# Two-layer hybrid diffusion block: modulation sums tied to the product's pace, rotary tables moved into the FFN, branch A's keys and queries first

## The chip, the cores and the metric

The kernel runs on one core of a Trainium2 chip. The metric is device time in microseconds (us), lower is better. Five engines work side by side, each in its own order: TensorE (PE in the profile) multiplies, VectorE (DVE) and ScalarE (ACT) do elementwise work, GpSimd (POOL) does small elementwise work and copies, SyncE (SP) issues the DMAs.

## The reference, cut to what matters

Two layers over 256 latent and 256 context tokens of width 1024. Each layer is an FFN half step, three token mixers, and a second FFN half step; every norm is modulated by sums over the conditioning vector.

```python
for l in range(DEPTH):                       # 2
    mx = split(silu(c) @ ada_w[l] + ada_b[l], 9)       # modulation of the latents, mz alike of the context
    x = x + 0.5 * mx[2] * swiglu(adaln(x, ffn1_norm, mx[0], mx[1]), ffn1_w_in, ffn1_w_out)   # z alike
    u = adaln(x, mix_norm, mx[3], mx[4])               # A: windowed GQA, B: global GQA, C: latent attention
    ya, yb, yc = A(u), B(u), C(u)                      # queries and keys: rms norm per head, gains, rotary
    m = sigmoid(ga) * (ya @ w_a) + sigmoid(gb) * (yb @ w_b) + sigmoid(gc) * (yc @ w_c)
    x = x + mx[5] * (m @ w_out)
    x = x + 0.5 * mx[8] * swiglu(adaln(x, ffn2_norm, mx[6], mx[7]), ffn2_w_in, ffn2_w_out)
return x                                     # the last layer's second half does the latents only
```

## The kernel before

All 512 tokens are the columns of every product (256 in the last layer's second part). An fp32 product is three passes on TensorE (`mm3`, L101 to L103): each operand is split into a high part (ACT, L108) and a low part (DVE, L109). Weights come as chunks of 512 KB, two chunks ahead; every second one goes into a `q4` buffer, whose load waits for a one-element copy on GpSimd (L154).

TensorE's order is written by hand in the code's order of products; the order of the other engines comes from the framework's scheduler, and each engine runs its instructions strictly in that order.

An FFN half step (`ffn`, `residual`) makes the 22 row blocks of the hidden layer in three splits (7, 7, 8). A row block is a gate and an up product, 24 TensorE products of 512 columns each. `evac` then takes them out: silu on ACT, L495 on DVE (h = silu x up), the high half on ACT (L108, `m<-w`), the low half on DVE (L109, `m<-w,m`). After each split, `residual` multiplies its row blocks by the output weights and adds into x (L427); after the last split it also sums squares for the next norm (ACT L355, DVE L356), whose sum over channels is TensorE's L372.

The modulation of later stages is made under three of the FFNs (`ada`): a step loads 128 rows of `ada_w` (L249, 512 KB, tiles `pth` and `ptl`) and sums them against the conditioning with one DVE instruction per stream (L266, 128x1024, two per step, 224 in all; the FFN of layer 0 does 48 steps). A step comes after every 29 or 44 TensorE products (`PACE`). The load is issued three steps ahead of its use (`ADA_LOOK`) and waits for a copy on GpSimd (L248) of `self.pace`, an element of the newest low half of the hidden layer or of x. The sums themselves carry no such tie: the scheduler decides where they stand on DVE.

The mixer starts with `rope_tables` (loads of the gains, L580 and L584; DVE L585 to L599; GpSimd L594 and L606). Then come the keys and values of A and B (`prep_kv`: split of V, preparation of A's keys, of B's keys), then A's queries. `k_heads` (L666 on TensorE, L671 and L673 to split) turns keys, `q_heads` (L683) queries; scores are L706, the probabilities are turned by L750. A filler (gates and other branches' products) is handed out in estimated us by the table `FILLS` between these steps: `keys` before A's keys are turned, `start` before attention, `a` and `b` between scores.

Of the kernel before, what the change touches and what calls it, by code (L numbers as in the profile page):

```python
# [9 lines left out]
ALU = mybir.AluOpType  # L10
# [16 lines left out]


FILLS = (
    dict(a=2.0, b=1.7, keys=0.0, start=8.0, latent=2.0, ups=5.0, c0=9.0, c=2.5),  # L30
    dict(a=2.0, b=1.8, keys=7.5, start=8.0, latent=0.0, ups=2.0, c0=0.0, c=1.3),
)
ADA_LOOK = 3
DEPTH_AB, DEPTH_C = 3, (2, 3)
# [24 lines left out]
class Kernel:  # L59
# [171 lines left out]
    def ada(self, mods):  # L231


        nc = self.nc
        cb = self.T("m5", [128, 2, D])
        for i in range(2):
            nc.gpsimd.tensor_copy(out=cb[:, i, 0:1], in_=self.pace)
        nc.sync.dma_start(out=cb, in_=self.t["condb"])
        nc.scalar.activation(out=cb, in_=cb, func=AF.Silu)
        junk = self.T("m6", [128, 2, D])  # L240
        todo = [(l, m, j) for l, m in mods for j in range(KD)]
        raws = []

        def load():
            n = len(raws)
            if n < len(todo):
                raw = self.T(("pth", "ptl")[n % 2], [128, D], bufs=2)
                nc.gpsimd.tensor_copy(out=raw[:, 0:1], in_=self.pace)  # L248
                nc.sync.dma_start(out=raw, in_=self.t["ada_t"][todo[n]])  # L249
                raws.append(raw)  # L250


        for _ in range(ADA_LOOK):
            load()
        yield
        n = 0
        for l, m in mods:

            streams = 1 if l == DEPTH - 1 and m > 4 else 2
            o = self.mods[l][:, m]  # L260
            for j in range(KD):
                load()
                raw = raws[n]
                n += 1
                for i in range(streams):
                    nc.vector.scalar_tensor_tensor(  # L266
                        out=junk[:, i], in0=raw, scalar=1.0, in1=cb[:, i], op0=ALU.mult, op1=ALU.mult,
                        accum_out=o[:, j, i:i + 1])
                if j < KD - 1:
                    yield  # L270
            b = self.adab[:, l, m].unsqueeze(2).to_broadcast([128, KD, streams])
            nc.vector.tensor_tensor(out=o[:, :, :streams], in0=o[:, :, :streams], in1=b, op=ALU.add)
            self.set_gains(l, m, slice(0, KD), streams)
            yield
# [204 lines left out]
    def ffn(self, l, f, halves, fill, after):  # L479
# [18 lines left out]
        for si, (t0, nt) in enumerate(SPLITS):  # L498
            hid = [[self.T(f"m{i}", [128, 4, NT], F32R) for i in ii] for ii in ((0, 1), (3, 4))]
            i0 = 0  # L500
            if si == 0:
                held = []
                i0 = len(halves)
                for i in range(i0):
                    tag = self.turn()
                    held.append([(self.P(tag), self.chunk("ffn_in", (f, l, t0 + i, gu), 1024)) for gu in range(2)])
                if self.first:
                    self.first(sum(held, []), rhs)
                    self.first = None
                    for i in range(i0):  # L510
                        evac(i, hid, held[i][0][0], held[i][1][0], whole)
                else:
                    for half in halves:

                        for k in range(KD):
                            for acc, wt in sum(held, []):
                                self.col_product(wt, KD, rhs, acc, HALF[half], (k, k + 1))
                            if k % 2:
                                self.tick()
                        for i in range(i0):  # L520
                            evac(i, hid, held[i][0][0], held[i][1][0], HALF[half])
                        self.finish()
            for i in range(i0, nt):
                accs = []
                tag = self.turn()
                for gu in range(2):
                    acc = self.P(tag)
                    self.col_product(self.chunk("ffn_in", (f, l, t0 + i, gu), 1024), KD, rhs, acc, whole)
                    accs.append(acc)
                    if gu == 0:  # L530
                        fill(24)
                evac(i, hid, accs[0], accs[1], whole)
                self.pace = hid[1][i // 4][:, i % 4, 0:1].bitcast(F32)
                fill(24)
            hrhs = [[hid[s][k // 4][:, k % 4] for k in range(nt)] for s in range(2)]

            def weights(d, t0=t0, nt=nt):
                return self.chunk("ffn_out", (f, l, d, slice(None), slice(t0, t0 + nt)), nt * 128)

            final = si == len(SPLITS) - 1  # L540
            self.residual(l, n, weights, nt, hrhs, halves, final, fill, after if final else None)
# [104 lines left out]
        elif rq is None:  # L646
            self.gain_heads(t, c0, nh, 64)

    def prep_kv(self, raw):
        V = self.V = self.T("m6", [128, 4, 4, 128], F32R)  # L650
        for tt in range(4):
            v = raw[tt][:, 256:512].rearrange("p (h d) -> p h d", h=4)
            self.split(V[:, tt, :, 0:64], V[:, tt, :, 64:128], v)
        for b, c0 in enumerate((G_AK, G_BK)):
            if b:
                self.rope_tables64((c0,))
            for tt in range(4):
                self.prep_heads(raw[tt][:, b * 128:(b + 1) * 128].rearrange("p (h d) -> p h d", h=2), c0, tt, 2)

    def k_heads(self, raw, b):  # L660

# [126 lines left out]
                    lambda g=g, i=i: [v[g * 64:g * 64 + 64, i, HALF[half]] for v in y],  # L788
                )

    def attention(self, steps, preps, fill, depth):


        n = len(steps)
# [2 lines left out]
        for k in early:  # L797
            for f in preps[k]:
                f()
        for i in range(min(depth, n)):  # L800
            fill()
            steps[i][0]()
# [203 lines left out]
    def mixer(self, l, last, after):  # L1006
# [11 lines left out]
                self.tick()  # L1018
            self.finish()

        self.rope_tables(l)

        nc.scalar.activation(out=self.small("go", 1), in_=self.hh[:, KD - 1, 0:1].bitcast(F32), func=AF.Exp, scale=0.0)
        self.rq = [self.T(f"rq{b}", [128, 4, 8]) for b in range(3)]
# [7 lines left out]
        for k in range(KD):  # L1032
            s = self.dram.tile([128, NT], F32, name=f"xd{l}_{k}")
            nc.sync.dma_start(out=s[:, :nh], in_=self.x[k][:, whole])
            xd.append(s)
        self.prep_kv(g3)
        aq = self.T("m3", [128, 4, 512])
        aq = [aq[:, tt] for tt in range(4)]
        drain(self.tok_product(l, "w_aq", 512, 2, aq, qtts))
        for tt in qtts:  # L1040
            self.prep_heads(aq[tt].rearrange("p (h d) -> p h d", h=8), G_AQ, tt, 8, self.rq[0][:, tt])
        self.share = 3
        depth = DEPTH_AB
        y = [[self.T(f"m{i}", [128, 4, NT], F32R) for i in (0, 1)], []]
# [16 lines left out]
        def fill():  # L1061
            def gates(ds):
                for d in ds:
                    m.append(self.T(f"x{d}", [128, NT]))
                    yield from self.gate_tanh(l, 0, d, whole, m[d][:, whole])

            yield from gates(range(2))
            self.K[1] = self.k_heads(g3, 1)
            self.rope_tables64((G_BQ,))
            yield from gates(range(2, 4))  # L1070
            bq.extend(self.raw4(512))
            yield from self.tok_product(l, "w_bq", 512, 2, bq, qtts, "d")
            left = list(qtts)
# [32 lines left out]
        fill(us["keys"])  # L1106
        self.K[0] = self.k_heads(g3, 0)
        fill(us["start"] - us["keys"])
        self.attention(steps, preps, lambda: fill(us["a"] if self.at < na else us["b"]), depth)
        t3 = [self.T("q4", [128, 2, NT], F32R, bufs=Q4) for _ in range(3)]  # L1110
        qT = [[t3[s][:, 0], t3[s][:, 1], t3[2][:, s]] for s in range(2)]
        while not have:
# [265 lines left out]
```

## Time and profile before

| | before |
|---|---|
| median of 3 runs | 2191.96 us (2191.35 to 2192.39) |
| profiled execution, its own time | 2207.8 us |
| its span | 2206.0 us |
| TensorE busy | 2118.2 us (96%) |
| VectorE busy | 1490.1 us (68%) |
| ScalarE busy | 991.6 us (45%) |
| GpSimd busy | 523.0 us (24%) |
| mean granted TensorE clock | 0.985 |

The span is the time from the first to the last instruction. By the first instruction of each stage the FFN of layer 0 runs from about 29 to 416 us, its mixer to 928, its second FFN to 1300, the first FFN of layer 1 to 1663, its mixer to about 2006, and the last FFN to the end.

### The profile page before, as it was taken

Reading aid. Unit: us, or ns where it says so; the run is one execution under the profiler, and the core shown is the slowest. Engines: PE = TensorE matmul, PEld = TensorE weight load, DVE = VectorE, ACT = ScalarE, POOL = GpSimd, SP = SyncE. Lnnn points to the kernel's source line nnn. Section 1 sums busy time; section 2 is a strip of 40 time slices with the busy share of each in tenths; the row PEclk is TensorE's granted clock in tenths of the full one; section 3 lists DMA queues with packets and bytes.
Section 4 is the critical chain, followed back from the end, with each engine's and each line's share of the span. In section 5 each row is a group of like instructions: output and inputs, shape, how many; then the busy total and the mean of one; then the engine's idle time right before and its main releaser. Section 6 shows DMA issues by size and latency. Waiting matters only on the chain. (4 is left out here: it accounts for less than half of the span.)

```text
span 2206.0 us, 33338 instructions
## 1 busy us (share of the span) xinstructions
PE 2118.2 (96%) x11832; PEld 1840.0 (83%) x11832; DVE 1490.1 (68%) x3041; ACT 991.6 (45%) x2026; POOL 523.0 (24%) x806
## 2 busy tenths in 40 slices
PE   6999998999999999999999999999999799899999
PEld 3878787878898888988878898787887799799999
DVE  5676666678888665657665466755557978887665
ACT  4322222456775664432223343222235676675554
POOL 3100010365335431201000021010115633721000
PEclk9999999999999999999999999999999899999999
DMA  8554454331112213345544325455552332335554
GB/s 288 181 178 162 164 180 140 115 96 49 51 50 86 85 58 125 106 139 177 166 148 154 113 77 185 168 168 167 173 169 95 121 99 83 102 125 188 185 184 124
DMA packets 95526, 299.16 MB, mean 136 GB/s; under 512 B 10880, under 2 KB 15616, under 8 KB 94976
## 3 DMA queue, kind: packets, MB, share of 16 engines
q1 hardware_dynamic: 95360, 297.04, 41.4%
q8 instruction: 93, 1.52, 0.3%
q14 instruction: 73, 0.60, 0.1%
HBM read 292.80 MB, written 4.19 MB: 135 GB/s over the span
## 5 line engine op out<-in xcount | busy, mean ns | idle before, releaser
L108 ACT ACTIVATE whi<-raw 128x512 fp32r<-128x512 f32 (+2 forms) x521 | 310.0, 609 | 340.9 <-PE pd L102 96.5
L109 DVE TENSOR_TENSOR wlo<-raw,whi 128x512 fp32r<-128x512 f32 (+2 forms) x441 | 304.8, 695 | 87.5 <-ACT whi L108 85.7
L101 PE MATMUL pd<-hh,whi 128*128 128x512 f32 (+1 forms) x864 | 306.4, 355 | 3.3 <-ACT hh L408 1.9
L102 PE MATMUL pd<-hl,whi 128*128 128x512 f32 (+1 forms) x864 | 303.7, 352 | 0.9 <-DVE hl L409 0.9
L103 PE MATMUL pd<-hh,wlo 128*128 128x512 f32 (+1 forms) x864 | 302.8, 350 | 0.0
L108 ACT ACTIVATE whi<-q 128x512 fp32r<-128x512 f32 (+1 forms) x299 | 179.3, 615 | 230.2 <-PE pd L102 67.3
L154 POOL COPY q<-start 1x1 f32<-1x1 f32 x151 | 63.1, 418 | 818.8 <-DVE wlo L109 623.5
L109 DVE TENSOR_TENSOR wlo<-q,whi 128x512 fp32r<-128x512 f32 (+1 forms) x299 | 200.1, 673 | 79.4 <-ACT whi L108 78.2
L266 DVE SCALAR_TENSOR_TENSOR m<-ptl,m 128x1024 f32<-128x1024 f32 x112 | 134.5, 1222 | 165.2 <-DMA ptl<-ada_t 165.1
L266 DVE SCALAR_TENSOR_TENSOR m<-pth,m 128x1024 f32<-128x1024 f32 x112 | 134.6, 1222 | 159.4 <-DMA pth<-ada_t 144.7
L108 ACT ACTIVATE m<-w 128x512 fp32r<-128x512 f32 (+1 forms) x92 | 51.5, 560 | 351.4 <-DVE w L495 351.3
L101 PE MATMUL pd<-m,whi 128*128 128x256 f32 (+1 forms) x522 | 179.0, 343 | 15.5 <-ACT m L108 14.1
L101 PEld LDWEIGHTS pd<-hh,whi 128*128 128x128 f32 x864 | 165.5, 192 | 26.8 <-ACT hh L408 2.3
L102 PEld LDWEIGHTS pd<-hl,whi 128*128 128x128 f32 x864 | 165.4, 191 | 21.8 <-DVE hl L409 1.8
L103 PEld LDWEIGHTS pd<-hh,wlo 128*128 128x128 f32 x864 | 165.3, 191 | 21.2
L101 PE MATMUL pv<-hh,whi 128*128 128x512 f32 (+1 forms) x512 | 182.3, 356 | 0.0
L102 PE MATMUL pv<-hl,whi 128*128 128x512 f32 (+1 forms) x512 | 182.2, 356 | 0.0
L103 PE MATMUL pv<-hh,wlo 128*128 128x512 f32 (+1 forms) x512 | 182.2, 356 | 0.0
L102 PE MATMUL pd<-m,whi 128*128 128x512 f32 (+1 forms) x530 | 181.5, 342 | 0.6 <-DVE m L109 0.4
L103 PE MATMUL pd<-m,wlo 128*128 128x256 f32 (+1 forms) x522 | 177.9, 341 | 0.0
L101 PE MATMUL ps<-hh,whi 128*128 128x512 f32 (+1 forms) x480 | 169.3, 353 | 1.1 <-DVE w L495 1.1
L102 PE MATMUL ps<-hl,whi 128*128 128x512 f32 (+1 forms) x480 | 168.3, 351 | 0.0
(322 smaller groups left out, 5085.8 us busy)
## 6 DMA issues: line engine op xcount, KB each, us to landing
q<-ffn_in SPq DMA_DIRECT2D x86, 512.0 KB, 3.7
raw<-ffn_in SPq DMA_DIRECT2D x86, 512.0 KB, 4.3
pth<-ada_t SPq DMA_DIRECT2D x64, 512.0 KB, 4.8
ptl<-ada_t SPq DMA_DIRECT2D x64, 512.0 KB, 5.2
raw<-w_gate SPq DMA_DIRECT2D x48, 512.0 KB, 3.5
q<-ffn_out SPq DMA_DIRECT2D x32, 448.0 KB, 3.4
raw<-ffn_out SPq DMA_DIRECT2D x32, 448.0 KB, 3.8
raw<-w_br SPq DMA_DIRECT2D x41, 256.0 KB, 2.6
```

The source lines that it names most:

```text
L101: mm(out, lhsT=ah, rhs=bh, start=first, stop=False)
L102: mm(out, lhsT=ah, rhs=bl, start=False, stop=False)
L103: mm(out, lhsT=al, rhs=bh, start=False, stop=last)
L108: self.nc.scalar.activation(out=hi, in_=src, func=AF.Copy)
L109: (eng or self.nc.vector).tensor_tensor(out=lo, in0=src, in1=hi.bitcast(F32), op=ALU.subtract)
L154: nc.gpsimd.tensor_copy(out=raw[0:1, 0:1], in_=self.start)
L266: nc.vector.scalar_tensor_tensor(out=junk[:, i], in0=raw, scalar=1.0, in1=cb[:, i], op0=ALU.mult, op1=ALU.mult, accum_out=o[:, j, i:i + 1])
```

## The change

1. Every step of the modulation sums first makes a 128x1 tile `go` on GpSimd from `self.pace` (at least 1 and at most 1, so 1.0), and the two DVE sums of the step take it as their factor in place of the constant 1.0. That is 112 more GpSimd instructions; DVE, ACT and TensorE have as many as before.
2. `rope_tables` is called in the first FFN half step, at its second split, and no longer at the mixer's start.
3. `prep_kv` is parted. A's keys come first, then A's query product and its preparation, then the split of V. B's keys are prepared in the filler behind the first gate and turned behind the fourth (before: turned behind the second).
4. `FILLS`: a new lead of 3 us of filler stands between the queries' turning and the first scores; `start` goes from 8 to 9 and from 8 to 10; in layer 1 `keys` goes from 7.5 to 3.

```diff
@@ FILLS
-    dict(a=2.0, b=1.7, keys=0.0, start=8.0, latent=2.0, ...
-    dict(a=2.0, b=1.8, keys=7.5, start=8.0, latent=0.0, ...
+    dict(a=2.0, b=1.7, keys=0.0, start=9.0, q=3.0, latent=2.0, ...
+    dict(a=2.0, b=1.8, keys=3.0, start=10.0, q=3.0, latent=0.0, ...
@@ ada
+                go = self.small("go", 1)
+                nc.gpsimd.tensor_scalar(out=go, in0=self.pace, scalar1=1.0, scalar2=1.0, op0=ALU.min, op1=ALU.max)
                 for i in range(streams):
                     nc.vector.scalar_tensor_tensor(
-                        out=junk[:, i], in0=raw, scalar=1.0, in1=cb[:, i], op0=ALU.mult, op1=ALU.mult,
+                        out=junk[:, i], in0=raw, scalar=go, in1=cb[:, i], op0=ALU.mult, op1=ALU.mult,
                         accum_out=o[:, j, i:i + 1])
@@ ffn
+            if si == 1 and f == 0:
+                self.rope_tables(l)
@@ attention(steps, preps, fill, depth, lead=lambda: None)
         for k in early:
             for f in preps[k]:
                 f()
+        lead()
@@ mixer
-        self.rope_tables(l)
...
-        self.prep_kv(g3)
+        self.prep_k(g3, 0)
         (A's query product and its preparation)
+        self.prep_v(g3)
@@ fill, in mixer
-            yield from gates(range(2))
-            self.K[1] = self.k_heads(g3, 1)
+            yield from gates(range(1))
+            self.prep_k(g3, 1)
+            yield from gates(range(1, 4))
+            self.K[1] = self.k_heads(g3, 1)
             self.rope_tables64((G_BQ,))
-            yield from gates(range(2, 4))
```

**The end of a split of an FFN (layer 0, second split), VectorE.** `pth` and `ptl` are loaded rows of the modulation weights, `q` and `raw` chunks of FFN weights, `w` is h, `m` the hidden layer, `pv` the last row block's up product. Before:

```order
L109 TENSOR_TENSOR m_262_1326<-w_1831,m_260_1324 128x512
L109 TENSOR_TENSOR wlo_1928<-raw_1925,whi_1927 128x512
L109 TENSOR_TENSOR wlo_1932<-raw_1925,whi_1931 128x384
L266 SCALAR_TENSOR_TENSOR m_137_657,mods_85<-pth_1835,m_136_652 128x1024 x2
L109 TENSOR_TENSOR wlo_1940<-q_379_1936,whi_1939 128x512
L495 TENSOR_TENSOR w_1915<-p_1913,pv_1877 128x512
L109 TENSOR_TENSOR wlo_1944<-q_379_1936,whi_1943 128x384
L109 TENSOR_TENSOR m_262_1326<-w_1915,m_260_1324 128x512
```

And now, at the same row block (lines of the changed kernel are three to ten higher: L269 is the sum, L498 h):

```order
L109 TENSOR_TENSOR m_276_1354<-w_1902,m_274_1352 128x512
L269 SCALAR_TENSOR_TENSOR m_137_657,mods_85<-ptl_1766,go_1909,m_136_652 128x1024 x2
L109 TENSOR_TENSOR wlo_2003<-raw_2000,whi_2002 128x512
L275 TENSOR_TENSOR mods_85<-mods_85,adab 128x16
L109 TENSOR_TENSOR wlo_2007<-raw_2000,whi_2006 128x384
L324 SCALAR_TENSOR_TENSOR G_87<-mods_85,gn 128x16
L109 TENSOR_TENSOR wlo_2015<-q_411_2011,whi_2014 128x512
L498 TENSOR_TENSOR w_1988<-p_1986,pv_1950 128x512
L109 TENSOR_TENSOR wlo_2019<-q_411_2011,whi_2018 128x384
L109 TENSOR_TENSOR m_276_1354<-w_1988,m_274_1352 128x512
```

Before, the sums ahead of the last h read a load that is issued in the same row block (`pth_1835`, behind `w_1831`). Now they read one that is issued some two row blocks earlier (`ptl_1766`, named ahead of `w_1902` and `w_1988`). On GpSimd that stretch now reads:

```order
L154 COPY q_411_2011<-start_342 1x1
L248 COPY pth_1724<-m_275_1353 128x1
L267 TENSOR_SCALAR go_1727<-m_275_1353 128x1
L267 TENSOR_SCALAR go_1769<-m_275_1353 128x1
L248 COPY ptl_1766<-m_275_1353 128x1
L154 COPY q_427_2117<-start_342 1x1
L248 COPY pth_1815<-m_276_1354 128x1
L267 TENSOR_SCALAR go_1818<-m_276_1354 128x1
L267 TENSOR_SCALAR go_1860<-m_276_1354 128x1
L248 COPY ptl_1857<-m_276_1354 128x1
```

The load `ptl_1766` and the `go` that lets it be used (`go_1909`, behind these rows) lie three steps apart, and each `go` stands behind a copy L154 for the FFN's weights.

**The end of the first FFN of layer 0, VectorE.** `x` is the residual, `yt` the running sum of squares, `gt` and `gc` the gains. Before:

```order
L427 SCALAR_TENSOR_TENSOR x_5_99<-pv_3103,gate_89,x_5_99 128x256
L588 TENSOR_SCALAR gt_3436<-gt_3436 128x128
L585 TENSOR_SCALAR gc_3439<-gc_3439 128x2
L586 TENSOR_SCALAR gc_3439<-gc_3439 64x1
L588 TENSOR_SCALAR gt_3436<-gt_3436 128x128
L588 TENSOR_SCALAR gt_3436<-gt_3436 128x64
L599 TENSOR_SCALAR nsink_3459<-gt_3436 128x8
L356 TENSOR_TENSOR yt_2990<-yt_2990,w_3174 128x256
```

And now:

```order
L269 SCALAR_TENSOR_TENSOR m_137_657,mods_85<-pth_3024,go_3170,m_136_652 128x1024 x2
L359 TENSOR_TENSOR yt_3103<-yt_3103,w_3163 128x256
L359 TENSOR_TENSOR yt_3106<-yt_3106,w_3167 128x256
L430 SCALAR_TENSOR_TENSOR x_4_97<-ps_3174,gate_89,x_4_97 128x256 x2
L109 TENSOR_TENSOR wlo_3244<-q_650_3236,whi_3243 128x512
L430 SCALAR_TENSOR_TENSOR x_5_99<-pv_3224,gate_89,x_5_99 128x256
L269 SCALAR_TENSOR_TENSOR m_137_657,mods_85<-ptl_3116,go_3218,m_136_652 128x1024 x2
L359 TENSOR_TENSOR yt_3103<-yt_3103,w_3211 128x256
```

The gains' rows are gone from the place; the last two steps of the modulation sums, which ran earlier, stand there. In layer 1 the last sums (one stream each) stand there in the same way.

**Branch A's start in the mixer of layer 1, TensorE.** `vh` and `th` are raw keys and values, `m_3340` and `m_3448` raw queries, `hh` and `hl` the normalised input times which the gates' weights (`whi`, `wlo`) are taken. Before, where B's keys and then A's queries are turned:

```order
L102 MATMUL pd_16198<-hl_15447,whi_16114 128x256
L103 MATMUL pd_16198<-hh_15446,wlo_16115 128x256
L666 MATMUL pt_16234<-ident,vh_15654 128x128
L666 MATMUL pt_16234<-ident,vh_15655 128x128
L666 MATMUL pt_16234<-ident,vh_15656 128x128
L666 MATMUL pt_16234<-ident,th_15657 128x128
L101 MATMUL pd_16249<-hh_15446,whi_16147 128x256
L102 MATMUL pd_16249<-hl_15447,whi_16147 128x256
L103 MATMUL pd_16249<-hh_15446,wlo_16148 128x256
L683 MATMUL pt_16263<-ident,m_3340_15987 128x128 x4
L101 MATMUL pd_16249<-hh_15446,whi_16147 128x256
```

And now, where A's queries and then B's keys are turned (L690 is the queries', L673 the keys'):

```order
L101 MATMUL pd_16488<-hh_15725,whi_16407 128x256
L102 MATMUL pd_16488<-hl_15726,whi_16407 128x256
L103 MATMUL pd_16488<-hh_15725,wlo_16408 128x256
L690 MATMUL pt_16523<-ident,m_3448_16183 128x128 x4
L673 MATMUL pt_16535<-ident,vh_15910 128x128
L673 MATMUL pt_16535<-ident,vh_15911 128x128
L673 MATMUL pt_16535<-ident,vh_15912 128x128
L673 MATMUL pt_16535<-ident,th_15913 128x128
L101 MATMUL pd_16595<-whi_16454,hh_15725 128x512
L102 MATMUL pd_16595<-wlo_16455,hh_15725 128x512
L103 MATMUL pd_16595<-whi_16454,hl_15726 128x512
```

B's keys stood three products ahead of the queries, on the same pair of `t` buffers of PSUM, and 24 products behind A's keys. Now the queries stand 66 products behind A's keys, B's keys follow them, and 24 products of 512 columns lie between them and the first scores (before 21 of 256).

## Rows read from the trace of the kernel before

**Rows 1.** The page's line of busy time by engine, and the view of clocks.

```profile
PE 2118.2 (96%) x11832; PEld 1840.0 (83%) x11832; DVE 1490.1 (68%) x3041; ACT 991.6 (45%) x2026; POOL 523.0 (24%) x806
core 0: 2206.0 us, clock 0.985
```

**Rows 2.** The view of waits, TensorE: us in all, times, longest us.

```profile
PE pd L101 <- ACT m L108: 14.1, 4, 5.1
...
PE pt L372 <- DVE yt L356: 9.1, 5, 4.0
PE pt L683 <- DVE m L673: 6.9, 1, 6.9
PE ps L706 <- DVE q L109: 5.7, 2, 4.2
PE ps L101 <- ACT m L108: 5.0, 2, 3.6
PE pt L750 <- DVE ptl L109: 3.4, 2, 2.7
```

**Rows 3.** The view of waits, VectorE, the modulation sums.

```profile
DVE m L266 <- DMA ptl<-ada_t: 165.1, 41, 6.9
...
DVE m L266 <- DMA pth<-ada_t: 144.7, 42, 6.2
```

**Rows 4.** The timeline at the second split's end, layer 0: start, duration, engine.

```profile
241.36 1.23 DVE L266 SCALAR_TENSOR_TENSOR m<-pth,m 128x1024 f32<-128x1024 f32 x1 [4.64 <-DMA pth<-ada_t]
...
244.27 0.68 DVE L495 TENSOR_TENSOR w<-p,pv 128x512 f32<-128x512 f32 x1
...
245.64 0.69 DVE L109 TENSOR_TENSOR m<-w,m 128x512 fp32r<-128x512 f32 x1 [0.23 <-ACT m L108]
...
245.66 0.79 PE L101 MATMUL pd<-m,whi 128*128 128x512 f32 x1 [5.13 <-ACT m L108]
...
246.45 0.53 POOL L248 COPY ptl<-m 128x1 f32<-128x1 f32 x1 [0.80 <-POOL q L154]
...
247.83 0.63 PE L102 MATMUL pd<-m,whi 128*128 128x512 f32 x1
...
248.26 0.63 PE L103 MATMUL pd<-m,wlo 128*128 128x512 f32 x1
```

**Rows 5.** The table by stretches: busy us (instructions) by engine, granted clock, DMA.

```profile
128.00:246.00 118.00, 112.87 (x497) 92.98 (x496) 81.84 (x147) 30.40 (x55) 10.98 (x27) 0.99 0.51 170
246.00:373.00 127.00, 123.71 (x535) 101.62 (x534) 83.57 (x150) 32.24 (x59) 11.56 (x29) 0.98 0.50 166
373.00:416.00 43.00, 36.36 (x198) 31.23 (x198) 25.93 (x57) 12.57 (x27) 5.39 (x15) 0.91 0.42 131
416.00:443.00 27.00, 26.28 (x144) 22.93 (x145) 20.32 (x49) 16.63 (x31) 14.23 (x18) 0.89 0.30 98
...
1664.00:1690.00 26.00, 24.21 (x138) 21.03 (x138) 19.41 (x46) 14.81 (x27) 12.99 (x17) 0.93 0.18 61
...
1710.00:1731.00 21.00, 12.06 (x93) 11.41 (x92) 20.16 (x37) 12.45 (x25) 16.91 (x19) 0.87 0.44 139
1731.00:1764.00 33.00, 29.44 (x167) 26.21 (x167) 28.95 (x57) 22.95 (x51) 20.69 (x19) 0.91 0.34 106
```

**Rows 6.** The timelines at the ends of three FFNs, in order of time.

```profile
410.40 0.52 DVE L588 TENSOR_SCALAR gt<-gt 128x128 f32<-128x128 f32 x1 [2.77 <-DMA gt<-gains]
...
927.89 0.58 PE L372 MATMUL pt<-ones,yt 128*128 128x1 f32 x4 [1.14 <-DVE yt L356]
...
1653.58 0.87 DVE L427 SCALAR_TENSOR_TENSOR x<-pv,gate,x 128x256 f32<-128x256 f32 x2
1654.11 0.18 POOL L579 COPY gt<-x 128x1 f32<-128x1 f32 x1 [10.37 <-DVE x L427]
...
1657.51 0.52 DVE L588 TENSOR_SCALAR gt<-gt 128x128 f32<-128x128 f32 x1 [1.40 <-DMA gt<-gains]
...
1663.44 0.61 PE L372 MATMUL pt<-ones,yt 128*128 128x1 f32 x4 [2.48 <-DVE yt L356]
```

More of the change, by code (lines that the diff above doesn't have):

```diff
@@ L29 @@
 FILLS = (
-    dict(a=2.0, b=1.7, keys=0.0, start=8.0, latent=2.0, ups=5.0, c0=9.0, c=2.5),
-    dict(a=2.0, b=1.8, keys=7.5, start=8.0, latent=0.0, ups=2.0, c0=0.0, c=1.3),
+    dict(a=2.0, b=1.7, keys=0.0, start=9.0, q=3.0, latent=2.0, ups=5.0, c0=9.0, c=2.5),
+    dict(a=2.0, b=1.8, keys=3.0, start=10.0, q=3.0, latent=0.0, ups=2.0, c0=0.0, c=1.3),
 )
@@ L647, in prep_heads, with prep_v @@
             self.gain_heads(t, c0, nh, 64)
-    def prep_kv(self, raw):
+    def prep_v(self, raw):
         V = self.V = self.T("m6", [128, 4, 4, 128], F32R)
@@ L653, in prep_kv, with prep_k @@
             self.split(V[:, tt, :, 0:64], V[:, tt, :, 64:128], v)
[L654 to L658, printed above, removed]
+    def prep_k(self, raw, b):
+        c0 = (G_AK, G_BK)[b]
+        if b:
+            self.rope_tables64((c0,))
+        for tt in range(4):
+            self.prep_heads(raw[tt][:, b * 128:(b + 1) * 128].rearrange("p (h d) -> p h d", h=2), c0, tt, 2)
     def k_heads(self, raw, b):
@@ L789, in gqa, with attention @@
                 )
-    def attention(self, steps, preps, fill, depth):
+    def attention(self, steps, preps, fill, depth, lead=lambda: None):
         n = len(steps)
@@ L1108, in mixer @@
         fill(us["start"] - us["keys"])
-        self.attention(steps, preps, lambda: fill(us["a"] if self.at < na else us["b"]), depth)
+        self.attention(steps, preps, lambda: fill(us["a"] if self.at < na else us["b"]), depth, lambda: fill(us["q"]))
         t3 = [self.T("q4", [128, 2, NT], F32R, bufs=Q4) for _ in range(3)]
```

## The prediction, made before the changed kernel ran

> **What bounds the kernel now.** I read the page's busy line first [rows 1]: TensorE is busy 2118.2 us of the span of 2206.0, 96%. The number of products stays, so a change can win in two places only: the span's idle time on TensorE (2206.0 - 2118.2 = 88 us), and products that run at a low granted clock. The mean clock is 0.985, and (1 - 0.985) x 2206 = 33 us is what a low clock costs if TensorE works meanwhile.
>
> The view of waits says what the idle time waits for [rows 2]. The four waits of `pd` and the two of `ps` for ACT's `m` (14.1 and 5.0 us) are the same event: a split of an FFN ends, and the first output products need the hidden layer's last row block. The timeline shows why [rows 4]. VectorE waits 4.64 us, until 241.36, for the DMA of a row of modulation weights, then runs two sums, and behind them, in its own order, stands L495, which makes h. It starts at 244.27; ACT and TensorE follow, and TensorE has stood 5.13 us. The sum is not urgent at all, it only stands ahead of an urgent instruction. Over the kernel these waits come 83 times, 309.8 us in all [rows 3], mostly hidden. In the timeline a wait of 4 to 6 us of VectorE for such a load stands ahead of each of those six stops, as in the one shown.
>
> The clock follows the stops. Behind the 5.13 us the products come 0.43 us apart (247.83 to 248.26, [rows 4]), against 112.87 / 497 = 0.227 us in the stretch before [rows 5]: the granted clock was at its lower level, 1.2 GHz. A stretch's loss is (1 - clock) x length [rows 5]: 0.02 x 127 = 2.5 us for 246 to 373, 0.09 x 43 = 3.9 for 373 to 416 (two stops, and a third begins), 0.11 x 27 = 3.0 for 416 to 443, 0.07 x 26 = 1.8 for 1664 to 1690, 0.13 x 21 = 2.7 for 1710 to 1731, 0.09 x 33 = 3.0 for 1731 to 1764.
>
> The third look is at what ends the other long stops: at the ends of the first FFNs L372 waits for VectorE's `yt` (4.0 us longest, 2.48 in layer 1, against 1.14 at the end of the mixer of layer 0, where no gains are loaded [rows 2, 6]); in layer 1's mixer the queries' turning L683 waits 6.9 us for L673, the split of the turned keys; in layer 0's the first scores wait 4.2 us.
>
> **The change, part by part.**
>
> *Ties on the sums.* A load waits for the pace of its step, its use now for the pace three steps later: 3 x 29 x 0.227 = 20 us, against a longest wait for such a load of 6.9 us [rows 3]. So no sum should wait for a DMA where the scheduler has kept this distance, and at the split's end the order shows h behind a sum of an old load. I strike the six stops: 14.1 + 5.0 = 19.1 us, and the clock behind them: 2.5, then 3.2 of the 3.9 (the rest belongs to the stop at 416), and 1.8 each for the two long stops of the later FFNs (their clock has no row here; the stop of 2.48 us cost 1.8). 19.1 + 2.5 + 3.2 + 3.6 = 28.4 us.
>
> The price is the wait for `go`. The pace is VectorE's own low half. A GpSimd copy of it starts 0.12 us after its end (245.64 + 0.69 to 246.45, [rows 4]) and takes 0.18 us beside a VectorE instruction that reads PSUM (1654.11 inside L427), 0.53 us beside one with two SBUF inputs (246.45 inside L109) [rows 4, 6]. One copy and one `go` then keep VectorE 0.6 to 1.3 us per step. It has that: from 128 to 246 it was busy 81.84 of 118 us [rows 5], 36 idle, which is 36 / (118 / 10.9) = 3.3 us per row block (48 x 0.227 = 10.9 us) or 3.3 / (48 / 29) = 2.0 us per step. Hidden, so 0, with bounds of 0 and some 10 us (below). The 112 `go` are at most 112 x 0.53 = 59 us on GpSimd, which is busy 523 of 2206. The factor read from SBUF instead of a constant has no row; it lies on VectorE, in the same 2.0 us.
>
> The row says that such a small GpSimd instruction is slower beside VectorE's two-input work. The Trainium skill, GPSIMD Engine Reference, section Specifications, says that GpSimd's SBUF interfaces are shared with VectorE and contend with its instructions of two SBUF inputs; this agrees with the 0.18 and 0.53, and as the sums themselves have two SBUF inputs, a `go` may by it sit out one whole sum (1.23 us). By the rule a step would cost VectorE up to 0.12 + 0.53 + 1.23 = 1.9 us instead of 1.3, just what is free: by the one and by the other the gain stays 45 us.
>
> *Rotary tables.* At the ends of the first FFNs L588 held VectorE 2.77 us in layer 0 and 1.40 in layer 1 for the gains' DMA [rows 6], and five small instructions follow. They go. But sums that ran earlier now stand there: two of 1.23 us in layer 0 right behind `x_5`, one in layer 1. So layer 1 should come down from 2.48 to 1.14 (1.3 us, and the clock's 1.8), layer 0 only half of 4.0 - 1.14 (1.4) and half of the 3.0 of clock (1.5): 6.0 us, bounds 0 and 9. At their new place the gains' wait holds VectorE as long, where TensorE has its next row blocks' products ahead; nothing there needs h sooner than a row block.
>
> *Branch A first, layer 1.* L683 waited for L673 because B's and A's turned keys held both `t` buffers of PSUM while VectorE was busy 20.16 of 21 us [rows 5]. In the new order 66 products stand between A's keys and the queries and B's keys come behind, so the 6.9 us go; but B's keys must then be prepared in time, and VectorE's work in the stretch is the same but for the tables. I take 2 back: 4.9. Of the clock's 2.7 + 3.0 I take 3.5 and of L750's 3.4 a half, 1.7; TensorE idled 21 - 12.06 = 8.9 us from 1710 to 1731, so 2.0 beyond the 6.9 (A's keys are late for L666); as A's keys now come first I count these in full: 12.1 us. Bounds 0 (VectorE bound, the stop moves) and 18.
>
> *Branch A first, layer 0.* The scores' 4.2 us: a lead of 3 us of filler now stands there. With 1.8 for the clock 6.0; I take 4.5, bounds 0 and 6.
>
> *What is given back.* `FILLS` hands out the same filler earlier, so it lacks later: in layer 1 a product of the latent branch (30 products of 288 columns, 30 x 0.227 x 288 / 512 = 3.8 us) no longer covers a wait for VectorE at that place. I count 3, and 3 for new small waits of `go` and of the keys that I can't place: 6 in all, bounds 0 and 12.
>
> Sum: 28.4 + 6.0 + 12.1 + 4.5 - 6 = 45 us. The profiled execution took 2207.8 us, 15.8 above the median; I carry the difference over: 2191.96 - 45 = 2147.
>
> **The rivals.**
>
> *The FFNs gain, the mixers don't.* VectorE is busy 20.16 of 21 and 28.95 of 33 us in layer 1's mixer [rows 5]; a reordering there takes no work from it, and B's keys, made later, may stop the filler. Then 28.4 + 6.0 - 3 = 31, 2161 us. For it: those two rows. Against it: TensorE waited for buffers there, not for the last of VectorE's work.
>
> *Sums still wait for their DMA.* If the loads slip as `go` do (both stand in GpSimd's one order, each behind an L154 that waits for VectorE), the distance shrinks and h stays behind a wait. Then only 6.0 + 12.1 + 4.5 - 6 = 17 us remain: 2175. For it: L154, L248 and `go` stand in one row in the order. Against it: 20 us against 6.9.
>
> *Slower: VectorE falls behind.* The round from VectorE over GpSimd back to VectorE comes at each step. It decides at 2.0 us per step; beyond it each us lengthens a row block by 48 / 29 = 1.66 us, and 3 FFNs with sums have 66. At 3 us per step that is 1.0 x 1.66 x 66 = 110 us against the 45: 2191.96 + 65 = 2257; 0.45 us over the limit already eats the gain. For it: two-input work beside nearly every `go`. Against it: VectorE stands idle while it waits, so `go` has the SBUF to itself.
>
> *More than forecast.* All stops named go, nothing comes back: 28.4 + 9 + 18 + 6 = 61, 2131.
>
> **How the numbers follow.** The forecast, 2147 with its own range of 2137 to 2157, gets 0.48; the FFNs alone (2157 to 2168) 0.20; sums that still wait (2168 to 2188) 0.14; all and nothing back 0.10; slower 0.08. From 2128 to 2178 I leave out the slower case, about 0.06 of the third and 0.02 below. Changes within 0.2% (4.4 us) can't be told from none: about 0.05 of the third case falls there. Faster 0.87, same 0.05, slower 0.08.
>
> **What would show it.** In the new profile the sums' wait for `pth` and `ptl` should be almost gone, a wait for `go` of about 1 us standing in its place; `pd` and `ps` for ACT's `m` near 0; the granted clock 1.00 from 246 to 416 us. L372's waits near 1.1 to 2.5 us. No stop of L690 (before L683) over 2 us. Wrong it would be if VectorE's wait for `go` comes to over 2 us a step or h stands late at all row blocks, if L713's or L673's waits grow by what L683's shrink, or if the sums that now stand in the FFN's end hold `yt` as long as the gains did.

## The result, and the profile after

The changed kernel takes 2168.02 us (median of 4 runs, 2167.43 to 2170.04) against 2192.18 us before in the same comparison: a ratio of 0.9879, 95% interval 0.9846 to 0.9913, so 1.2% faster. Forecast were 2147 us, with a range of 2128 to 2178. The direction and the range held; the gain is 24 us by the medians where I had 45, and the time lies above the forecast's own band of 2137 to 2157. Below, a stop is a time in which TensorE stands idle.

The page's busy line and the view of clocks, changed kernel (they answer to [rows 1]):

```profile
PE 2099.1 (97%) x11832; PEld 1829.1 (84%) x11832; DVE 1519.1 (70%) x3041; ACT 1008.9 (47%) x2026; POOL 537.1 (25%) x934
...
core 0: 2165.3 us, clock 0.992
```

The same number of products takes 19 us less of TensorE, and the granted clock is 0.992 in place of 0.985. The view of waits, TensorE and then VectorE (us in all, times, longest):

```profile
PE pv L766 <- DVE ptl L109: 5.1, 6, 2.1
PE pt L673 <- DVE vh L627: 3.9, 1, 3.9
PE pd L101 <- ACT x L975: 3.1, 1, 3.1
PE pt L673 <- DVE v L118: 3.1, 1, 3.1
PE pt L870 <- DVE q L109: 2.9, 1, 2.9
PE ps L713 <- DVE q L109: 2.7, 2, 1.4
PE pt L375 <- DVE yt L359: 2.7, 3, 1.1
...
DVE m L269 <- POOL go L267: 25.3, 56, 0.5
```

The waits of `pd` and `ps` for ACT's `m` (19.1 us, [rows 2]) and the 309.8 us for the loads of the sums [rows 3] are gone: no sum waits for a load any more. The squares' wait (L375, L372 before) is down from 9.1 to 2.7 us. In their place stand waits of the mixers: L673 turns keys, L766 multiplies probabilities with values, L870 turns queries of the latent branch.

The timeline at the second split's end in layer 0, which answers to [rows 4]:

```profile
229.72 0.39 PE L101 MATMUL pd<-m,whi 128*128 128x512 f32 x1
...
229.92 0.69 DVE L498 TENSOR_TENSOR w<-p,pv 128x512 f32<-128x512 f32 x1 [1.45 <-PE pv L103]
...
231.31 0.69 DVE L109 TENSOR_TENSOR m<-w,m 128x512 fp32r<-128x512 f32 x1 [0.23 <-ACT m L108]
...
232.12 0.19 POOL L248 COPY ptl<-m 128x1 f32<-128x1 f32 x1 [0.80 <-POOL q L154]
...
232.27 0.19 POOL L267 TENSOR_SCALAR go<-m 128x1 f32<-128x1 f32 x1
...
232.49 1.28 DVE L269 SCALAR_TENSOR_TENSOR m<-pth,go,m 128x1024 f32<-128x1024 f32 x1 [0.48 <-POOL go L267]
```

The first output product runs without a wait. VectorE now waits for the product (1.45 us) ahead of the last h, not the product for VectorE. The round over GpSimd, from the end of the low half (231.31 + 0.69 = 232.00) to the sum, is 0.49 us.

The table by stretches of the changed kernel (columns as in [rows 5]); the first three answer to 246 to 443 there, the last two to 1710 to 1764:

```profile
246.00:360.00 114.00, 114.00 (x504) 94.39 (x504) 85.78 (x143) 36.04 (x59) 15.57 (x45) 1.00 0.56 181
360.00:391.00 31.00, 31.00 (x195) 28.11 (x195) 24.04 (x51) 9.81 (x20) 1.29 (x5) 1.00 0.32 101
391.00:417.00 26.00, 25.51 (x153) 21.89 (x152) 21.23 (x53) 17.95 (x33) 15.23 (x19) 1.00 0.32 102
...
1670.00:1691.00 21.00, 13.86 (x101) 13.15 (x99) 18.32 (x29) 13.30 (x27) 17.77 (x18) 0.86 0.45 134
1691.00:1724.00 33.00, 26.70 (x150) 22.91 (x151) 25.56 (x57) 18.93 (x42) 20.11 (x20) 0.88 0.31 98
```

From 246 us on layer 0's first FFN is now full, at the full clock. Layer 1's mixer still has its stops, and the timeline says where:

```profile
1678.71 0.58 PE L101 MATMUL pd<-hh,whi 128*128 128x256 f32 x1 [3.11 <-ACT x L975]
...
1689.60 0.45 PE L673 MATMUL pt<-ident,vh 128*128 128x128 f32 x1 [3.07 <-DVE v L118]
...
1693.95 0.48 PE L673 MATMUL pt<-ident,vh 128*128 128x128 f32 x1 [3.91 <-DVE vh L627]
```

L690 (the queries) waits no more; the first row is a gate product, and the other two are B's keys, which are late now.

By stages, us, one profiled execution each, read off the timeline. A stage runs from a norm's last sum over channels (the second half's first L372, whose line is a few higher in the other kernels) to the next norm's, so the norm stands with the stage ahead of it. The first stage begins with the first sum of the first norm, the last one ends with the last product:

| kernel | FFN1, layer 0 | mixer 0 | FFN2, layer 0 | FFN1, layer 1 | mixer 1 | last FFN |
|---|---|---|---|---|---|---|
| before | 416.2 | 495.0 | 372.4 | 380.4 | 325.8 | 196.4 |
| before, second profile | 412.2 | 494.7 | 369.3 | 379.6 | 324.0 | 196.4 |
| changed | 388.4 | 500.1 | 366.4 | 367.9 | 326.1 | 196.5 |
| ties only | 388.1 | 495.1 | 366.4 | 367.8 | 323.0 | 196.4 |
| ties and tables | 386.8 | 495.0 | 366.4 | 367.8 | 324.9 | 196.4 |
| all but the ties | 411.4 | 500.7 | 367.6 | 372.1 | 327.2 | 196.4 |
| ties, tables, new order, old fillers | 388.5 | 492.1 | 366.4 | 368.0 | 332.7 | 196.5 |
| ties, tables, old order, new fillers | 386.9 | 502.3 | 366.3 | 367.8 | 324.8 | 196.5 |
| new order in layer 0 only, old fillers | 385.6 | 493.0 | 366.4 | 368.0 | 322.8 | 196.4 |

From before to the changed kernel the three FFNs with sums give back 27.8 + 6.0 + 12.5 = 46.3 us, and the mixers take 5.1 + 0.3 of it. For these three stages together the table by stretches has, before and then changed:

```profile
sum 1168.93, PE 1133.46 PEld 942.33 DVE 719.95 ACT 363.21 POOL 155.88; mean PE 377.82 PEld 314.11 DVE 239.98 ACT 121.07 POOL 51.96
sum 1122.70, PE 1114.67 PEld 932.25 DVE 749.12 ACT 379.88 POOL 168.40; mean PE 371.56 PEld 310.75 DVE 249.71 ACT 126.63 POOL 56.13
```

So TensorE's idle time falls from 35.5 to 8.0 us, and its busy time by 18.8 us.

### The profile page after: what moved, and what is told of

It reads as the page before. It is cut to its first block, busy times and chain, and to the rows that moved or that the text cites. A ratio compares the mean times of both kernels' runs of the same rounds, so it can differ in the third digit from the quotient of the medians.

```text
span 2165.3 us, 33481 instructions
## 1 busy us (share of the span) xinstructions
PE 2099.1 (97%) x11832; PEld 1829.1 (84%) x11832; DVE 1519.1 (70%) x3041; ACT 1008.9 (47%) x2026; POOL 537.1 (25%) x934
## 4 chain that ended last, share of the span: by engine, by line
PE 85%; DVE 7%; POOL 3%; DMA 2%; issue 2%; ACT 1%; SPq 0%; POOLq 0%; ACTq 0%; DVEq 0%
PE pd L101 12%; PE pd L102 12%; PE pd L103 12%; PE pv L103 7%; PE pv L101 7%; PE pv L102 7%; PE ps L101 7%; PE ps L102 7%; PE ps L103 7%; PE ps L713 2%; PE pt L757 2%; DVE wlo L109 1%; POOL w L410 1%; PE pv L766 1%; PE pv L765 1%
## 5 line engine op out<-in xcount | busy, mean ns | idle before, releaser
L108 ACT ACTIVATE whi<-raw 128x512 fp32r<-128x512 f32 (+2 forms) x521 | 314.5, 611 | 470.9 <-PE pd L102 138.3
L108 ACT ACTIVATE whi<-q 128x512 fp32r<-128x512 f32 (+1 forms) x299 | 184.2, 620 | 378.8 <-PE pd L102 101.9
L154 POOL COPY q<-start 1x1 f32<-1x1 f32 x151 | 54.8, 363 | 655.0 <-DVE wlo L109 474.1
L103 PE MATMUL ps<-hh,wlo 128*128 128x512 f32 (+1 forms) x480 | 168.3, 351 | 0.0
L269 DVE SCALAR_TENSOR_TENSOR m<-pth,go,m 128x1024 f32<-128x1024 f32 x112 | 140.1, 1280 | 23.0 <-POOL go L267 13.0
L269 DVE SCALAR_TENSOR_TENSOR m<-ptl,go,m 128x1024 f32<-128x1024 f32 x112 | 140.0, 1280 | 12.3 <-POOL go L267 12.3
```

Of the source, the lines that this page charges most:

```text
L103: mm(out, lhsT=al, rhs=bh, start=False, stop=last)
L108: self.nc.scalar.activation(out=hi, in_=src, func=AF.Copy)
L154: nc.gpsimd.tensor_copy(out=raw[0:1, 0:1], in_=self.start)
L269: nc.vector.scalar_tensor_tensor(out=junk[:, i], in0=raw, scalar=go, in1=cb[:, i], op0=ALU.mult, op1=ALU.mult, accum_out=o[:, j, i:i + 1])
```

## The experiments

Each kernel had its expectation on record before it ran: a theory, and a rival with another time. "Before" in a ratio is the kernel before, run in the same comparison.

**The kernel before, once more.**

> The kernel before, unchanged, for a second profile. Theory (the profile shown before the prediction was of a slower execution than the 2192 us of the runs, and part of its stops at the ends of the FFNs' splits come and go between executions): this profile's own time is near 2192 and the waits of pd and ps for ACT's m come to some 5 to 12 us in place of 19.1, with little half clock from 246 to 416 us. Rival (the profiler itself makes an execution 15.8 us longer, evenly): the time is again near 2208 and the six stops are all there.

It took 2198.5 us, between theory and rival. Its waits (columns as above):

```profile
PE pd L101 <- ACT m L108: 12.2, 4, 5.2
PE pt L372 <- DVE yt L356: 6.9, 5, 3.6
PE ps L101 <- ACT m L108: 6.3, 3, 3.2
```

The stops are there again, 18.5 us against 19.1, where the theory had 5 to 12; but they are not the same ones: two of 1.8 and 1.6 us where there were 3.1 and 3.6, and a new one of 3.2 us at 1627. Within the three comparisons made for the experiments, the kernel before ran from 2182.43 to 2204.79 us in 43 runs; the profile that I argued from (2207.8) lies above them all. That the profiler adds 15.8 us evenly is not so.

**Only the ties.**

```diff
+                go = self.small("go", 1)
+                nc.gpsimd.tensor_scalar(out=go, in0=self.pace, scalar1=1.0, scalar2=1.0, op0=ALU.min, op1=ALU.max)
-                        out=junk[:, i], in0=raw, scalar=1.0, ...
+                        out=junk[:, i], in0=raw, scalar=go, ...
```

> Only the ties: each modulation sum takes its factor from the pace; rotary tables, key order and fillers as before. Theory (all of the gain is in the FFNs' splits, and is the ties'): 17 to 24 us faster than before, 2168 to 2175. Rival (the tables' move and the new order of branch A bring a good part, as I forecast): 8 to 15 us faster, 2177 to 2184.

2158.21 us, ratio 0.9831 (0.9808 to 0.9854): 36 us below the 2194.45 of before, more than theory and rival had, and 10 us under the whole change (between two comparisons; their profiles' spans are 2156.9 and 2165.3 us). The view of waits, TensorE and then VectorE:

```profile
PE pt L685 <- DVE m L675: 6.9, 1, 6.9
PE ps L708 <- DVE q L109: 5.7, 2, 4.2
...
PE pt L374 <- DVE yt L358: 2.7, 3, 1.1
...
DVE m L268 <- POOL go L266: 25.3, 56, 0.5
```

The waits for ACT's `m` are gone. The mixers stand as before, with their stops of 6.9 and 4.2 us. The ends of the first FFNs (L374) are mended too, with the tables where they were.

**All but the ties.** The changed kernel without the lines above.

> The changed kernel without the ties: tables moved, branch A first, new fillers, factor 1.0 again. Theory (the mixers give nothing net): within 6 us of before, 2186 to 2196, and L673 waits some 8 us for B's keys in layer 1. Rival (my forecast of 22.6 - 6 us for tables and mixers): 2173 to 2180.

2198.17 us, ratio 1.0016 (1.0003 to 1.0030): a loss of some 4 us, just past the theory's 2196. The view of waits, TensorE:

```profile
PE pd L101 <- ACT m L108: 12.8, 4, 5.4
...
PE ps L101 <- ACT m L108: 3.2, 2, 2.1
...
PE pt L373 <- DVE yt L357: 2.8, 4, 1.1
```

The waits for ACT's `m` stay. The squares' wait is down to 2.8 us here as well: the tables' move alone does that. By the table of stages the FFNs are 10 us shorter than in the second profile of before, and the mixers 9 longer. In sum the rest of the change is no gain.

**Ties and tables' move.**

```diff
+            if si == 1 and f == 0:
+                self.rope_tables(l)
...
-        self.rope_tables(l)
```

> Ties and the tables' move, branch A and fillers as before. Theory (the stop in front of L372 goes at the two ends of the first FFNs, and the new order of branch A is no gain): 2 to 6 us faster than the ties alone and equal to or faster than the whole change (2163 to 2169). Rival (the sums that now stand there hold the running squares as long as the gains did): equal to the ties alone within 2 us, and slower than the whole change.

2159.29 us, ratio 0.9841 (0.9818 to 0.9865): equal to the ties alone, as the rival had it, and 9 us under the whole change, as only the theory had it. But the rival's reason is not the one: with the ties alone the squares' sum (L372, there L374) has no stop left to win back.

**The fillers, and the order, apart.** The whole change with the fillers of before:

```diff
-    dict(..., keys=0.0, start=9.0, q=3.0, ...  /  keys=3.0, start=10.0, q=3.0
+    dict(..., keys=0.0, start=8.0, q=0.0, ...  /  keys=7.5, start=8.0, q=0.0
```

> The whole change with the fillers of before (start 8 and 8, keys 0 and 7.5, no lead). Theory (the new order of branch A alone is what costs: B's keys are prepared late and L673 waits for them): 2165 to 2172, the scores of layer 0 and L673 still wait. Rival (the new fillers cost, by leaving later steps of attention without products): 2155 to 2161, as the ties alone.

2164.74 us, ratio 0.9860 (0.9829 to 0.9891). And ties and tables with the old order of preparation, but the new fillers and the lead:

```diff
+    dict(..., keys=0.0, start=9.0, q=3.0, ...  /  keys=3.0, start=10.0, q=3.0
...
+        lead()
```

> Ties and tables' move, the keys and queries prepared in the order of before, but the new fillers with the lead of 3 us. Theory (the order of branch A costs, the fillers don't): 2155 to 2161, and the 4 us stop of the scores in layer 0 is gone. Rival (the fillers cost): 2164 to 2170, with new stops of 1 to 2 us in layer 0's attention between 510 and 710 us.

2165.28 us, ratio 0.9862 (0.9831 to 0.9893). Each alone costs some 7 us against a kernel with ties alone in the same comparison (2158.01, the next experiment), and neither theory is the whole. Against the row "ties and tables" in the table of stages, the new order wins 3 us in layer 0 and loses 8 in layer 1; the new fillers lose 7 in layer 0 and nothing in layer 1. The two don't add up: with the new fillers the new order costs 1.3 us in layer 1 (326.1 against 324.8). So the loss of the whole change in its mixers lies for the most part in layer 0 (500.1 against 495.0), and is the fillers'. It is where the second rival put it; the timeline of the second kernel, layer 0's attention, shows two stops that the ties alone don't have:

```profile
513.98 0.30 PE L754 MATMUL pt<-ident,p 128*128 128x128 f32 x1 [1.77 <-DVE ptl L109]
...
645.70 0.44 PE L763 MATMUL pv<-ptl,m 128*128 128x256 f32 x1 [2.08 <-DVE ptl L109]
```

**A tie one step behind the load.** `go` is made when the next row is loaded, one step after the sum's own load.

```diff
+                go = self.T("gos", [128, 1], bufs=6)          # in load()
+                nc.gpsimd.tensor_scalar(out=go, in0=self.pace, ...)
+                gos.append(go)
...
+                go = gos[min(n, len(todo) - 1)]               # n has been counted up
```

> Ties alone, but a sum is tied to the pace of one step behind its load (29 products, 6.6 us) in place of three steps (20 us). Theory (what counts is that the tie lies further behind the load than the load takes to land, about 5 us; the rest of the distance is spare): as the ties of three steps, 2157 to 2166, with waits for the load of 10 to 60 us in all, few of them 2 us or longer. Rival (the distance itself or the scheduler's order at three steps makes the gain): half of it at most, 2172 to 2190.

2158.01 us, ratio 0.9832 (0.9801 to 0.9862): the same as three steps. The view of waits, VectorE:

```profile
DVE m L270 <- DMA ptl<-ada_t: 29.1, 13, 3.8
...
DVE m L270 <- POOL gos L252: 23.5, 51, 0.8
DVE m L270 <- DMA pth<-ada_t: 22.0, 13, 3.9
```

51 us of waits for loads are left of 309.8, and no stop of TensorE for ACT's `m` comes of them. (The expectation had few of 2 us or longer: 11 of the 26 are.)

**A factor from SBUF, untied.**

```diff
-                        out=junk[:, i], in0=raw, scalar=1.0, ...
+                        out=junk[:, i], in0=raw, scalar=self.ones[:, 0:1], ...
```

> The kernel before with the factor read from a constant tile of ones in SBUF, tied to nothing. Theory (the gain is the tie's, and a factor from SBUF costs nothing that shows): equal to before within its scatter, 2187 to 2202, the sums wait some 300 us for their loads, and one sum takes as long as before within 0.05 us. Rival (the operand's form, or the order that follows from it, brings the gain): 2155 to 2180.

2205.72 us, ratio 1.0044 (1.0023 to 1.0065). The gain is the tie's, as the theory said. It was wrong that the factor costs nothing: a group of the sums reads, in the kernel before and then here,

```profile
L266 DVE SCALAR_TENSOR_TENSOR m<-ptl,m 128x1024 f32<-128x1024 f32 x112 | 134.5, 1222 | 165.2 <-DMA ptl<-ada_t 165.1
L266 DVE SCALAR_TENSOR_TENSOR m<-ptl,ones,m 128x1024 f32<-128x1024 f32 x112 | 140.9, 1281 | 151.8 <-DMA ptl<-ada_t 151.8
```

1281 ns each in place of 1222, 0.06 x 224 = 13 us more of VectorE, and this kernel is 9 us slower than before, past the theory's 2202.

**The new order in layer 0 only.** The kernel with ties, tables, the fillers of before, and the new order behind `if not l`.

```diff
+        if l:
+            self.prep_v(g3)
         self.prep_k(g3, 0)
+        if l:
+            self.prep_k(g3, 1)
...                                     # and the filler: of before in layer 1, new in layer 0
```

> Ties and tables' move; the new order of branch A in layer 0 only, layer 1 in the order of before, the fillers of before in both. Theory (order and fillers act by layer and add up: the order gives layer 0's mixer some 3 us with the old fillers and costs layer 1's some 8): 2153 to 2158, mixer of layer 0 some 478 us, of layer 1 some 324. Rival (the 3 us are scatter of one profile): 2157 to 2162, as the ties alone.

2155.26 us, ratio 0.9819 (0.9794 to 0.9844), the fastest here. The theory's stages came (mixers 479.3 us without the norm, and 322.8); that it beats the ties alone is 3 us between two comparisons, and the intervals overlap, so that is not shown.

**A's keys turned first in layer 1.** As the one above, with keys 4.5, start 4.5 and a lead of 3.5 in layer 1.

```diff
-    dict(a=2.0, b=1.8, keys=7.5, start=8.0, q=0.0, ...
+    dict(a=2.0, b=1.8, keys=4.5, start=4.5, q=3.5, ...
```

> As the version with the new order in layer 0 only, and in layer 1 the fillers are cut so that TensorE turns A's keys, then A's queries, then B's keys (keys 4.5, start 4.5, lead 3.5); all keys are prepared early, as before. Theory (L690's stop of 6.9 us in layer 1 stands because B's keys are turned ahead and hold a buffer while VectorE is full): the stop falls below 3 us and layer 1's mixer is 3 to 6 us shorter, 2149 to 2155. Rival (VectorE is the bound of that stretch, whatever the order): the stop moves to L673 or to the scores, layer 1's mixer is 322 to 327 us and the time equals that version within 2 us.

2160.79 us, ratio 0.9842 (0.9818 to 0.9867). The rival is right that the stop only moves, but had the time equal: it is 5.5 us longer, with layer 1's mixer at 327.7 us against 322.8. The queries are now asked for before VectorE has prepared them, and B's keys wait behind:

```profile
1672.43 0.45 PE L690 MATMUL pt<-ident,m 128*128 128x128 f32 x1 [7.04 <-DVE m L627]
...
1679.48 0.45 PE L673 MATMUL pt<-ident,vh 128*128 128x128 f32 x1 [4.41 <-DVE m L680]
```

**A long way to `go`.** Ties alone, with eight more dependent instructions per step.

```diff
+                for _ in range(8):
+                    nc.gpsimd.tensor_scalar(out=go, in0=go, scalar1=1.0, scalar2=1.0, op0=ALU.min, op1=ALU.max)
```

> Ties alone, and each `go` is passed through eight more GpSimd instructions of the same size, one behind the other, before the sums may use it. Theory (VectorE has about 2 us per step to spare under the FFNs): eight more take 1.5 to 4 us per step, so VectorE waits 1 to 3 us for `go` at most steps, the stops at the splits' ends come back in part, and the time is 2162 to 2200. Rival (the wait is covered whatever its length in this range): 2156 to 2162.

2160.45 us, ratio 0.9842 (0.9817 to 0.9867), some 2 us above the ties alone in the other comparisons. The groups of GpSimd and then the view of waits, VectorE:

```profile
L268 POOL TENSOR_SCALAR go<-go 128x1 f32<-128x1 f32 x1024 | 244.9, 257 | 40.6
...
DVE m L270 <- POOL go L268: 91.5, 68, 2.5
```

1024 / 8 = 128 steps, not the 112 that I had counted: 32 of them have one sum. 8 x 0.257 = 2.1 us more per step make VectorE wait 91.5 us in place of 25.3, and TensorE feels little of it: the squares' wait is 4.7 us in place of 2.7, and no stop for ACT's `m` comes back. That is the rival's side. By the mean VectorE waits 91.5 / 128 = 0.7 us a step, so the limit of 2.0 us that I had worked out was not reached.

**Fewer fillers in layer 1.** The whole change with the fillers of before in layer 0, and keys 3, start 6, no lead in layer 1.

```diff
-    dict(a=2.0, b=1.8, keys=7.5, start=8.0, q=0.0, ...
+    dict(a=2.0, b=1.8, keys=3.0, start=6.0, q=0.0, ...
```

> The whole change with the fillers of before in layer 0 and keys 3, start 6, no lead in layer 1, so that B's keys, prepared late as in the change, are turned behind the second scores. Theory (in layer 1 the new order costs because B's keys are asked for right behind their preparation): L673 waits under 2 us in layer 1 and its mixer takes 322 to 327 us, 2153 to 2160. Rival (the preparation's place on VectorE is what costs): layer 1's mixer stays at 329 us or more, 2160 to 2168.

2165.36 us, ratio 0.9862 (0.9837 to 0.9886), and layer 1's mixer is at 334.8 us, as the rival had it. What the order changes is seen in the first 33 us of layer 1's mixer and the 56 us behind, first for the kernel with the new order in layer 0 only (old order here), then for the whole change with old fillers (new order here); the third column of busy times is VectorE's:

```profile
1631.00:1664.00 33.00, 33.00 (x165) 27.94 (x164) 28.82 (x70) 20.28 (x43) 26.93 (x37) 1.00 0.27 82
1664.00:1684.00 20.00, 11.24 (x77) 10.83 (x76) 19.26 (x28) 13.40 (x25) 13.87 (x13) 0.78 0.42 131
1684.00:1720.00 36.00, 32.45 (x205) 29.06 (x205) 30.33 (x68) 25.49 (x59) 22.71 (x22) 0.98 0.37 116
```

```profile
1632.00:1665.00 33.00, 33.00 (x164) 27.92 (x163) 25.57 (x56) 19.90 (x40) 24.15 (x30) 1.00 0.29 83
1665.00:1685.00 20.00, 12.61 (x81) 11.49 (x80) 18.04 (x28) 12.52 (x26) 16.08 (x16) 0.84 0.48 154
1685.00:1721.00 36.00, 27.58 (x144) 23.26 (x144) 29.69 (x67) 21.23 (x47) 21.89 (x22) 0.83 0.24 75
```

While TensorE is full of products, the old order gives VectorE 28.8 of 33 us, the new one 25.6. The work left over for later is then asked for where TensorE waits for it: 32.45 against 27.58 us of TensorE in the third stretch, and a clock of 0.98 against 0.83.

## Why the prediction was right, and where its sizes were off

**Where it landed.** The range held, in part by luck. Between the two profiles the FFNs gave 11.9 us more than I had added up for them and the mixers 16.0 less, so that the sum of 45 came near the 40.7 us by which the spans differ. The time stands at the edge of two rivals' bands. The one below, by which the FFNs gain and the mixers don't, is what the stages show; the one above, by which sums still wait for their loads, is not: no sum does.

**The ties: right in mechanism, too small.** A sum that waits for its load no longer stands ahead of h; the six stops are gone, and the runs show that the tie alone does it (36 us by medians) and that a factor without a tie does not. For ties and tables together I had 28.4 + 6.0 = 34.4 us in these stages; the profiles show 46.3. Both parts were too small: TensorE's idle time there fell by 27.4 us, where I had 19.1 for the six stops and 2.7 for the squares'; its busy time fell by 18.8 us at as many products, where I had 9.3 + 3.3 = 12.6 for the clock. The tie also changes the order in which the scheduler puts VectorE's work; whether that order would do without the wait for `go` was not tried.

**The price of `go`: right.** It costs VectorE 0.45 us at the 56 of the 128 steps where it waits (25.3 / 56), under my 0.6 to 1.3; the copy and the `go` take 0.19 us each in the round shown above. The slower rival did not come: even 2.1 us more on GpSimd per step cost some 2 us in all. The Trainium skill, GPSIMD Engine Reference, section Specifications, has GpSimd share its SBUF interfaces with VectorE and contend with instructions of two SBUF inputs. The trace agrees: a copy beside such work took 0.53 us [rows 4], and two of the 128 `go` (1.17 and 1.24 us) sat out a whole sum, as here under the second FFN of layer 0:

```profile
988.33 1.27 DVE L269 SCALAR_TENSOR_TENSOR m<-pth,go,m 128x1024 f32<-128x1024 f32 x1
988.41 1.24 POOL L267 TENSOR_SCALAR go<-m 128x1 f32<-128x1 f32 x1
```

**The tables: right that the gains' wait goes, wrong as a term of its own.** The 6.0 us belong to the ties as well as to the move: with the ties alone the squares wait 2.7 us in all, with the move alone 2.8, after both edits 2.7. Two edits that each remove the same stop must not both be paid for it. How the ties free that end is seen in layer 0 of the kernel with ties alone. The gains' rows stand behind an x as before, but VectorE reaches them without a wait, where it waited 2.77 us [rows 6]:

```profile
381.96 1.27 DVE L268 SCALAR_TENSOR_TENSOR m<-ptl,go,m 128x1024 f32<-128x1024 f32 x1
...
384.24 0.20 DVE L590 TENSOR_SCALAR gt<-gt 128x128 f32<-128x128 f32 x1
```

A tied sum and the squares behind it now fill the time in which the gains land (GpSimd's own wait for them ends at 383.53). In layer 1 waits of 0.86 and 0.97 us are left there, and the squares' stop is gone all the same.

**Branch A first: the term that failed.** I had 12.1 + 4.5 - 6 = 10.6 us of gain and the mixers lost 5.4 us (profiles); against ties and tables the whole change loses some 9 us by the medians. I had read the order of the kernel before wrongly in layer 1, in the part on the change too: B's keys were turned first and A's three products ahead of the queries, not the other way round. But the step that failed in layer 1 is the reading of the 6.9 us as a wait for buffers that another order would free. VectorE was busy 20.16 of 21 us there [rows 5]; three different orders left stops of 7.0 + 4.4, 3.8 + 3.0 + 3.7 and 3.1 + 3.1 + 3.9 us in place of the 6.9. My first rival said it: a reordering takes no work from VectorE. The new order even takes time from it, as it leaves VectorE idle earlier (25.6 us of 33 busy against 28.8). In layer 0 the order wins 2 to 3 us; there it is the lead and the larger `start` that lose 7. That is the filler given back later, which I had counted at 3 us in layer 1 alone (L870's wait of 2.9 us, 1.8 before, is that one) and not in layer 0. Which of the two numbers costs it was not tried apart.

**Carrying over: the step that halved the result.** From profile to profile the change is 2207.8 - 2167.4 = 40 us, near my 45. I then took 45 from a median 15.8 us lower, as if the profile's excess had nothing to do with the stops. But the two profiles of the kernel before differ by 9.3 us, and 7.9 of these lie in the three FFNs with sums. So the 15.8 us were in part the very thing that the change removes. It fits that untied kernels scatter (2182 to 2205 before, 2195 to 2214 with the untied factor) and tied ones less (2156.95 to 2159.04, 2157.38 to 2159.09, in four and five runs). Which stops are missing in an execution near 2185 us no profile here shows.

## What to carry to other kernels

On an engine that runs in order, look at what stands ahead of an urgent instruction: tie work that nobody waits for to a moment when its data has landed. Here one step behind the load's issue was enough, and the round over GpSimd cost half a microsecond where it was waited for. Do not count two edits for the same stop. Expect little of reordering a stretch whose second engine is 96% busy: in each order tried in layer 1 stops stayed, under other names, and what helped was to give that engine work earlier, while the first one was full. When the profile is slower than the runs, ask how much of the excess is the thing being removed before you take the gain off the median.

## What the runs showed that I had not expected

A factor read from a 128x1 tile makes a sum of 128x1024 0.06 us longer than a constant (1281 against 1222 ns), and the untied kernel with such sums was 9 us slower. That its 13 us of VectorE are the reason was not tried apart from the order, which shifts a little too. And the kernels whose sums wait for DMAs vary by 8 to 22 us within a comparison (9 to 17 runs), the tied ones by 2 to 5 (4 or 5 runs). That the waits are the reason is not shown.
